# The merge's second branch evacuated inside its PSUM banks, not into SBUF tiles

## The chip, the cores and the metric

The kernel runs on one core of a Trainium2 chip. The metric is the device time of one execution in microseconds (us), the median over runs. The profile is taken by the hardware profiler from one execution. PE stands for TensorE, DVE for VectorE, ACT for ScalarE, POOL for GpSimd, SP for the queue that issues most DMAs. L1206 means line 1206 of the kernel before.

## The reference

Two layers of a hybrid backbone, all in fp32: 512 latent and 256 context tokens, 1024 model channels. Each layer has two parallel token mixers (a windowed attention A and a grouped-query attention B) that share one input projection. What matters here is the end of a layer, where both are merged:

```python
def _merge(a_att, b_att, a_z, b_z, g_a, g_b, w_o_a, w_o_b, w_out):
    o_a = (a_att * jax.nn.silu(a_z)) @ w_o_a
    o_b = (b_att * jax.nn.silu(b_z)) @ w_o_b
    merged = jax.nn.sigmoid(g_a) * o_a + jax.nn.sigmoid(g_b) * o_b
    return merged @ w_out
...
    out_x = _merge(a_att, b_att, a_z, b_z, g_a, g_b, w_o_a, w_o_b, w_out)
    x_new = x + gate_x * out_x
```

In layer 0 the context tokens go through the same merge; in layer 1 only the 512 latent tokens do. The output is the latent stream after layer 1.

## The kernel before, in words

**Products.** Every large product is made of fp32 operands that are split into a high and a low part (type fp32r): `hi` is a cast of the value, `lo` is the value minus `hi`. `mm3` then issues three matmuls for each block of 128 channels: hi by hi, and the two mixed products (L423, L424, L425). A product with a 512-column output over four blocks of channels is thus 12 matmuls, over eight blocks 24. `chan_proj` has a variant for operands that come late (L448, L449, L451): the products with the high part of the activations first, those with their low part behind them. Weights are loaded by SP into `raw` tiles; ACT casts them to `whi` (L393, L408), and DVE or POOL makes `wlo` (L396, L410), by turns.

**Merge.** The product with `w_o_b` has channels on the partitions: eight blocks f = 0 to 7, and for each the tokens in spans, 0 to 512 and 512 to 768 in layer 0 (16 chunks), 0 to 512 in layer 1 (8 chunks). Each chunk sums four blocks of input channels. The gate of branch B and the gated result of branch A (written in earlier chunks by `evac_a`, L694) lie in SBUF tiles `tg`; `tg_part(0, ...)` is A's, `tg_part(1, ...)` is B's. `evac_b` takes a chunk out of PSUM in four operations: L1206 on DVE multiplies the product by (1 + B's part), L1207 on DVE adds A's part, L1209 on ACT casts the sum to `mh`, L1210 on DVE subtracts to get `ml`. `mh` and `ml` are the operands of the product with `w_out`.

**Output.** That product has tokens on the partitions (six tiles of 128 tokens in layer 0, four in layer 1) and 512 columns at a time, in two halves n. `evac_o` multiplies it by the residual's gate (L1238) and adds it to the residual stream `xt` (L1240). In layer 1 the last tile's second half is made in two pieces of 256 columns (L1265 and L1267), each followed by its DMA out.

**PSUM.** In the merge six banks of 512 fp32 columns are used in turn: one named psf, five named psx (`psw` gives them out, psf at every sixth). A bank is given to its next chunk when the last operation that reads the old one is done. In layer 1 chunk 0 has psf, chunks 1 to 5 have psx, and chunk 6 has psf again.

**Order.** A scheduler orders the instructions of each engine from the program's text by its own estimate of times; each engine then takes its list strictly in turn and waits by semaphores. So an instruction that waits holds up all that stands behind it on its engine. What each engine does around the change is in the order rows below.

Of the kernel before, what the change touches and what calls it, by code (L numbers as in the profile page):

```python
# [7 lines left out]
F32 = mybir.dt.float32  # L8
# [4 lines left out]
ALU = mybir.AluOpType  # L13
# [38 lines left out]
def R(ap):  # L52
    return ap.bitcast(F32R)
# [7 lines left out]
def hybrid_kernel(es: ExitStack, tc, x, ctx, cvec, w_ada, w_ada0, small, gvec, w_in, w_o_a, w_o_b, w_out,  # L61
                  bias_int, bias_edge, rope, ident_d, out):
    nc = tc.nc
    V, S, G, T = nc.vector, nc.scalar, nc.gpsimd, nc.tensor
# [10 lines left out]
    def nm(s):  # L75
        uid[0] += 1
        return f"{s}_{uid[0]}"

    def big(name):
        return bigp.tile([128, 3072], F32, tag="big", name=nm(name))  # L80
# [12 lines left out]
    def open_ps(x=0, **kinds):  # L93

        if "es" in pm:
            pm["es"].close()
        pm["es"] = ExitStack()
        pm["n"], pm["i"], pm["v_for"] = x + 1, 0, ()
        if x:
            kinds["x"] = (x, 512)  # L100
        for kind, (bufs, cols) in kinds.items():
            ps_pool(pm["es"], kind, bufs, cols)
# [18 lines left out]
    def x_src(t):  # L121
        if t < 4:
            return x0[128 * t:128 * t + 128, :]
        return ctx0[(t - 4) * 128:(t - 3) * 128, :]
# [141 lines left out]
    def ada_steps(l, tiles, halves, nv, pool, queue=None):  # L266

        cb = {}

        def load(h):  # L270
            cb[h] = pool.tile([128, 2, 512], F32, tag="cb", name=nm("cb"), bufs=1)
            for v in range(nv):
                src = cd[8 * v + 4 * h:8 * v + 4 * h + 4].rearrange("k p -> (k p)").unsqueeze(0)
                nc.sync.dma_start(cb[h][:, v, :], src.to_broadcast([128, 512]))

        def load_tile(h, i):
            cb["w"] = pool.tile([128, 512], F32, tag="rawb", name=nm("rawb"), bufs=2)
            (queue or nc.sync).dma_start(cb["w"], w_ada[l, h, i])

        def dot(h, i, v):  # L280
            if v == 0:
                load_tile(h, i)
            w = cb["w"]
            o = w if v == nv - 1 else pool.tile([128, 512], BF16, tag="junk", name=nm("junk"), bufs=1)
            behind(ON_DVE, lambda: V.tensor_tensor_reduce(o, w, cb[h][:, v, :], 1.0, 0.0, ALU.mult, ALU.add,
                                                          asum[:, i, h, v:v + 1]))
        res = []
        for h in halves:
            res += [lambda h=h: load(h)] + [lambda h=h, i=i, v=v: dot(h, i, v) for i in tiles for v in range(nv)]
        return res  # L290
# [292 lines left out]
    def layer(l, hx, nxt, start):  # L583
# [67 lines left out]
        def hilo_tiles(name):  # L651
            return [big(name + part).rearrange("p (f n) -> p f n", f=4) for part in "hl"]

        def hilo(src, dst, fs, lo_eng=(G,), parts=((0, ntok),)):
            sv = src.rearrange("p (f n) -> p f n", f=4)
            for n0, n1 in parts:
                for f in fs:
                    S.copy(R(dst[0][:, f, n0:n1]), sv[:, f, n0:n1])
                    lo_eng[f % len(lo_eng)].tensor_tensor(R(dst[1][:, f, n0:n1]), sv[:, f, n0:n1], dst[0][:, f, n0:n1], ALU.subtract)
# [4 lines left out]
        def o_chunks(br, prepare, evac):  # L664

            src = (w_o_a if br == "a" else w_o_b)[l]
            act = lambda part, k: gated[br][part][:, k, :]
            res = []
            for i in range(4):
                st = {}  # L670

                def ld(i=i, st=st):
                    st["w"] = load_w2(src, 256 * i, 4, pool_lo if br == "b" and i == 0 else mix_lo)
                pieces = [lambda f=f, n0=n0, n1=n1, i=i, st=st:
                          chan_proj(st["w"], f, act, n0, n1, lambda f, a, b, ps: evac(2 * i + f, a, b, ps),
                                    3 if br == "b" and i == 0 and first else 0)
                          for f in range(2) for n0, n1 in spans]
                res.append((ld, ([prepare] if i == 0 and prepare else []) + pieces))
            return res
# [9 lines left out]
        def tg_part(c, f, n0, n1):  # L689
            return tg[2 * (f // 4) + c].rearrange("p (f n) -> p f n", f=4)[:, f % 4, n0:n1]  # L690
# [503 lines left out]
        with tc.tile_pool(name=f"mrg{l}", bufs=1, reuse_waits="tile") as mp:  # L1194
            open_ps(x=5)
            extra = lambda name: mp.tile([128, 3072], F32, tag="extra", name=nm(name))
            gv = mp.tile([128, nv, DM], F32, tag="gate", name=nm("gate"), bufs=1)
            for v in range(nv):
                src = gd[l][8 * v:8 * v + 8].rearrange("k p -> (k p)").unsqueeze(0)
                nc.sync.dma_start(gv[:, v, :], src.to_broadcast([128, DM]))  # L1200
            hilo(zb, gated["b"], [3], (V,), spans)
            mg = []

            def evac_b(f, n0, n1, ps):
                a, b = tg_part(0, f, n0, n1), tg_part(1, f, n0, n1)
                V.scalar_tensor_tensor(b, b, 1.0, ps, ALU.add, ALU.mult)  # L1206
                V.tensor_tensor(a, a, b, ALU.add)  # L1207
                hi, lo = [m[:, f % 4, n0:n1] for m in mg[f // 4]]
                S.copy(R(hi), a)  # L1209
                V.tensor_tensor(R(lo), a, hi, ALU.subtract)  # L1210
            chunks = o_chunks("b", None, evac_b)
            chunks[0][0]()
            for i in range(4):
                if i < 3:
                    chunks[i + 1][0]()
                if i % 2 == 0:
                    mg.append(hilo_tiles("m"))
                for piece in chunks[i][1]:
                    piece()

            nt = 6 if first else 4
            xv = [a.rearrange("p (t n) -> p t n", t=3) for a in (big("xt0"), extra("xt1"))]
            xts = []
            for t in range(nt):
                xt = xv[t // 3][:, t % 3, :]
                nc.sync.dma_start(xt, x_src(t) if first else xs1[128 * t:128 * t + 128, :])
                xts.append(xt)
            a_m = lambda part, k: mg[k // 4][part][:, k % 4, :]
            bg = ada_steps(1, range(16), (1,), 2, mp, G) + [lambda: ada_mod(1)] if first else []
            run(bg, 1)  # L1230
            per_bg = -(-len(bg) // nt)
            for n in range(2):
                w = load_w(w_out[l], 512 * n, 512, KT, mix_lo)

                def evac_o(t, ps, n=n):
                    cs = slice(512 * n, 512 * n + 512)
                    t1 = mp.tile([128, 512], F32, tag="t1", name=nm("t1"), bufs=2)
                    V.tensor_tensor(t1, ps, gv[:, 0 if t < 4 else 1, cs], ALU.mult)  # L1238
                    xt = xts[t]
                    V.tensor_tensor(xt[:, cs], xt[:, cs], t1, ALU.add)  # L1240
                    if not first:
                        nc.sync.dma_start(o_lat[16 * t:16 * t + 16][:, :, cs], xt[:, cs])
                    elif n == 1:
                        if t < 4:
                            G.dma_start(xs1[128 * t:128 * t + 128, :], xt)
                        late.append(lambda: make_hx(1, t, xt, nxt(), mp))
                late = []
                if first and n == 1:
                    hp["lag"] = 2
                for t in range(nt):  # L1250
                    if not first and n == 1 and t == nt - 1:
                        break
                    tok_proj(w, 512, a_m, t, evac_o)
                    run(bg, per_bg)
                    run(late, len(late))
                turn_late(0)
            if not first:

                for c0, c1 in ((0, 256), (256, 512)):
                    ws = [(hi[:, c0:c1], lo[:, c0:c1]) for hi, lo in w]  # L1260
                    cs = slice(512 + c0, 512 + c1)
                    ps = psw(c1 - c0)
                    tok_mm(ps, ws, c1 - c0, a_m, nt - 1, 0, KT)
                    t1 = mp.tile([128, 512], F32, tag="t1", name=nm("t1"), bufs=2)[:, :c1 - c0]
                    V.tensor_tensor(t1, ps, gv[:, 0, cs], ALU.mult)  # L1265
                    xt = xts[nt - 1]
                    V.tensor_tensor(xt[:, cs], xt[:, cs], t1, ALU.add)  # L1267
                    (nc.sync if c0 else S).dma_start(o_lat[16 * nt - 16:16 * nt][:, :, cs], xt[:, cs])


# [245 lines left out]
```

## Time and profile before

| | us |
|---|---|
| runs shown | 1102.42, 1097.99, 1101.49 |
| their median | 1101.49 |
| the profiled execution | 1097.34 |
| its span | 1095.5 |
| granted TensorE clock, mean | 1.0 |

| engine | busy us | share of the span |
|---|---|---|
| PE | 1066.4 | 97% |
| DVE | 757.7 | 69% |
| ACT | 613.6 | 56% |
| POOL | 438.5 | 40% |

A row of a timeline has the start of an instruction, its duration, the engine, the line, and output <- inputs by the names in the program; in brackets stands how long the engine was idle before it, and what released it. "x2" joins instructions of one kind. The duration of a matmul or a DVE operation includes its fill: two neighbours start closer together than one of them lasts (in the last merge DVE operations on 128x512 elements last 0.68 us and start 0.60 us apart). A group's row ends in "sum, mean ns | idle time before it, and what ended it". Where a wait is for a PSUM bank, the releaser is the last operation that read the bank before.

### The profile page before, as it was taken

To read this page: it belongs to the slowest core of one execution; us is meant where nothing else is said; L and a number is where in the kernel's file an instruction comes from. 1 tells how busy PE (TensorE), PEld (TensorE's weight loads), DVE (VectorE), ACT (ScalarE), POOL (GpSimd) and SP (SyncE) were. 2 spreads that over 40 slices of the span, in tenths; PEclk is the share of its full clock that TensorE was granted. 3 is DMA by queue.
4 is the path that set the end of the run, shared out by engine and by line. 5 is a ranking of instruction groups with operands and counts; after the bars stand their busy time and mean duration, and the time that the engine had idled before them with its cause. 6 is when DMAs were issued, how large, how long until landed. Compare 5 with 4: busy or idle time off the path is not lost. (4 is left out here: it accounts for less than half of the span.)

```text
span 1095.5 us, 17697 instructions
## 1 busy us (share of the span) xinstructions
PE 1066.4 (97%) x6032; PEld 882.3 (81%) x6032; DVE 757.7 (69%) x1630; ACT 613.6 (56%) x1256; POOL 438.5 (40%) x371
## 2 busy tenths in 40 slices
PE   8999999999999999998999999999999999999998
PEld 6688888788897888887788788888877888877777
DVE  5667889975388676665587885467997665677473
ACT  6464279777343477676141184444999346777420
POOL 1054235554247143354321445232455473444631
PEclk9999999999999999999999999999999999999999
DMA  9454325554544478789533542453455536889742
GB/s 371 159 172 148 92 66 110 130 144 115 166 147 128 122 180 215 164 256 239 198 114 108 182 131 72 136 163 105 127 146 129 152 107 170 192 261 225 201 154 77
DMA packets 236002, 171.83 MB, mean 157 GB/s; under 512 B 160140, under 2 KB 201864, under 8 KB 234248
## 3 DMA queue, kind: packets, MB, share of 16 engines
q1 hardware_dynamic: 228576, 156.31, 51.8%
q0 software_dynamic: 2368, 7.87, 2.3%
q10 hardware_dynamic: 4968, 6.53, 1.8%
q8 instruction: 47, 0.77, 0.3%
q14 instruction: 43, 0.35, 0.1%
HBM read 115.58 MB, written 17.32 MB: 121 GB/s over the span
## 5 line engine op out<-in xcount | busy, mean ns | idle before, releaser
L825 POOL TENSOR_TENSOR h<-p,h 128x256 f16<-128x256 f32 (+2 forms) x104 | 113.8, 1102 | 192.1 <-ACT h L824 141.5
L410 POOL TENSOR_TENSOR wlo<-raw,whi 128x512 fp32r<-128x512 f32 x70 | 97.3, 1392 | 132.2 <-ACT whi L408 113.0
L423 PE MATMUL psf<-hx,whi 128*128 128x512 f32 (+1 forms) x360 | 137.7, 382 | 1.6 <-DVE zt L614 1.2
L424 PE MATMUL psf<-hx,whi 128*128 128x512 f32 (+1 forms) x360 | 135.4, 376 | 0.0
L425 PE MATMUL psf<-hx,wlo 128*128 128x512 f32 (+1 forms) x360 | 135.3, 376 | 0.0
L408 ACT CAST whi<-raw 128x512 fp32r<-128x512 f32 x136 | 83.1, 621 | 73.6 <-DMA raw<-in_w_in_dram 50.5
L423 PE MATMUL psx<-whi,hx 128*128 128x512 f32 (+1 forms) x328 | 121.0, 372 | 0.0
L425 PE MATMUL psx<-whi,hx 128*128 128x512 f32 (+1 forms) x328 | 120.0, 367 | 0.0
L424 PE MATMUL psx<-wlo,hx 128*128 128x512 f32 (+1 forms) x328 | 119.7, 366 | 0.0
L396 POOL TENSOR_TENSOR wlo<-raw,whi 128x512 fp32r<-128x512 f32 x40 | 60.1, 1507 | 123.7 <-ACT whi L393 69.9
L393 ACT CAST whi<-raw 128x512 fp32r<-128x512 f32 x88 | 54.2, 623 | 91.7 <-PE psx L425 35.0
L496 POOL TENSOR_TENSOR ss<-ss,ehalf 128x8 f32<-128x8 f32 (+2 forms) x40 | 64.7, 1621 | 74.3 <-DVE ss L493 69.1
L824 ACT CAST h<-p 128x256 f16<-128x256 f32 (+2 forms) x136 | 81.5, 617 | 11.2 <-DMA vb<-h 4.8
L1154 DVE CUSTOM_DVE_ANT_0 p<-pss,vb 128x768 f32<-128x768 f32 x64 | 60.3, 954 | 31.0 <-PE pss L881 27.5
L423 PEld LDWEIGHTS psf<-hx,whi 128*128 128x128 f32 x360 | 67.8, 188 | 15.2 <-DVE zt L614 1.6
L410 DVE TENSOR_TENSOR wlo<-raw,whi 128x512 fp32r<-128x512 f32 x66 | 63.4, 963 | 23.6 <-ACT whi L408 23.3
L425 PEld LDWEIGHTS psf<-hx,wlo 128*128 128x128 f32 x360 | 67.8, 188 | 11.7
L424 PEld LDWEIGHTS psf<-hx,whi 128*128 128x128 f32 x360 | 67.9, 189 | 10.7
L1155 ACT ACTIVATE p<-pss,mx 128x768 f32<-128x768 f32 x64 | 57.6, 901 | 25.5 <-DVE mx L1154 25.1
L425 PEld LDWEIGHTS psx<-whi,hx 128*128 128x128 f32 x328 | 61.9, 189 | 10.2
L424 PEld LDWEIGHTS psx<-wlo,hx 128*128 128x128 f32 x328 | 62.0, 189 | 9.4
L423 PEld LDWEIGHTS psx<-whi,hx 128*128 128x128 f32 x328 | 61.8, 189 | 9.2 <-issue 0.2
(333 smaller groups left out, 2903.2 us busy)
## 6 DMA issues: line engine op xcount, KB each, us to landing
raw<-in_w_in_dram SPq DMA_DIRECT2D x168, 256.0 KB, 2.9
rawb<-in_w_ada_dram SPq DMA_DIRECT2D x48, 256.0 KB, 2.8
raw<-in_w_out_dram SPq DMA_DIRECT2D x32, 256.0 KB, 2.9
tg<-gs SPq DMA_DIRECT2D x4, 1536.0 KB, 8.8
rawx<-in_w_ada_dram SPq DMA_DIRECT2D x4, 1024.0 KB, 10.7
rawy<-in_w_ada_dram SPq DMA_DIRECT2D x4, 1024.0 KB, 9.4
gs<-zt ACTq DMA_DIRECT2D x16, 256.0 KB, 2.5
raw<-in_w_o_a_dram SPq DMA_DIRECT2D x16, 256.0 KB, 4.0
```

The costliest lines, as they stand in the source:

```text
L393: S.copy(hi[:, :n], raw[:, :n])
L396: e.tensor_tensor(lo[:, :n], raw[:, :n], F(hi[:, :n]), ALU.subtract)
L408: S.copy(hi, raw)
L410: lo_eng(i).tensor_tensor(lo, raw, F(hi), ALU.subtract)
L423: T.matmul(ps, lhs[0], rhs[0], start=first, stop=False)
L424: T.matmul(ps, lhs[0], rhs[1], start=False, stop=False)
L425: T.matmul(ps, lhs[1], rhs[0], start=False, stop=last)
L496: G.tensor_tensor(ss, ss, ehalf[:, :n], ALU.pow)
L824: S.copy(h[:, 0], p[:, :n])
L825: eng.tensor_tensor(h[:, 1], p[:, :n], h[:, 0], ALU.subtract)
L1154: V.tensor_tensor_reduce(p, pss, lift, -1.0, 3e38, ALU.add, ALU.min, mx[:, 0:1])
L1155: S.activation(p, pss, AF.Exp, bias=mx[:, 0:1], accum_out=r[:, i, e:e + 1])
```

## The change

`evac_b` no longer writes its results to the `tg` tiles in SBUF. L1206 writes the gated product back to the PSUM tile, L1207 adds A's part to it there, and the cast L1209 and the subtraction L1210 read the sum from there. In `evac_o` and in the two last pieces the product with the gate is written back to the PSUM tile, where a tile `t1` in SBUF was used, and the residual's addition reads it from there.

```diff
             def evac_b(f, n0, n1, ps):
                 a, b = tg_part(0, f, n0, n1), tg_part(1, f, n0, n1)
-                V.scalar_tensor_tensor(b, b, 1.0, ps, ALU.add, ALU.mult)
-                V.tensor_tensor(a, a, b, ALU.add)
+                V.scalar_tensor_tensor(ps, b, 1.0, ps, ALU.add, ALU.mult)
+                V.tensor_tensor(ps, ps, a, ALU.add)
                 hi, lo = [m[:, f % 4, n0:n1] for m in mg[f // 4]]
-                S.copy(R(hi), a)
-                V.tensor_tensor(R(lo), a, hi, ALU.subtract)
+                S.copy(R(hi), ps)
+                V.tensor_tensor(R(lo), ps, hi, ALU.subtract)
...
                 def evac_o(t, ps, n=n):
                     cs = slice(512 * n, 512 * n + 512)
-                    t1 = mp.tile([128, 512], F32, tag="t1", name=nm("t1"), bufs=2)
-                    V.tensor_tensor(t1, ps, gv[:, 0 if t < 4 else 1, cs], ALU.mult)
+                    V.tensor_tensor(ps, ps, gv[:, 0 if t < 4 else 1, cs], ALU.mult)
                     xt = xts[t]
-                    V.tensor_tensor(xt[:, cs], xt[:, cs], t1, ALU.add)
+                    V.tensor_tensor(xt[:, cs], ps, xt[:, cs], ALU.add)
...
                     tok_mm(ps, ws, c1 - c0, a_m, nt - 1, 0, KT)
-                    t1 = mp.tile([128, 512], F32, tag="t1", name=nm("t1"), bufs=2)[:, :c1 - c0]
-                    V.tensor_tensor(t1, ps, gv[:, 0, cs], ALU.mult)
+                    V.tensor_tensor(ps, ps, gv[:, 0, cs], ALU.mult)
                     xt = xts[nt - 1]
-                    V.tensor_tensor(xt[:, cs], xt[:, cs], t1, ALU.add)
+                    V.tensor_tensor(xt[:, cs], ps, xt[:, cs], ALU.add)
```

The scheduler gives another order at some places. In the rows, "waits DVE_49" is a wait on DVE's semaphore, and the number behind a name tells tiles apart. First, TensorE in layer 0, where the first branch's last product (psf_6046, with weights of `w_o_a`) ends and the second branch's chunks follow. Before:

```order
L425 MATMUL psf_6046<-gah_5411,wlo_5824 128x256
L423 MATMUL psx_6309<-gbh_6064,whi_6166 128x256 [waits DVE_49]
L424 MATMUL psx_6309<-gbl_6065,whi_6166 128x256
L425 MATMUL psx_6309<-gbh_6064,wlo_6168 128x256
...
L423 MATMUL psx_6340<-gbh_6064,whi_6248 128x512 [waits DVE_49]
L424 MATMUL psx_6340<-gbl_6065,whi_6248 128x512
L425 MATMUL psx_6340<-gbh_6064,wlo_6250 128x512
```

With the change:

```order
L425 MATMUL psf_6046<-gah_5411,wlo_5824 128x256
L448 MATMUL psf_6178<-gbh_6064,whi_6154 128x512 [waits DVE_49]
L449 MATMUL psf_6178<-gbh_6064,wlo_6156 128x512
...
L451 MATMUL psf_6178<-gbl_6065,whi_6154 128x512 x2
...
L425 MATMUL psf_6178<-gbh_6064,wlo_6162 128x512
L423 MATMUL psx_6309<-gbh_6064,whi_6166 128x256 [waits DVE_49]
L424 MATMUL psx_6309<-gbl_6065,whi_6166 128x256
L425 MATMUL psx_6309<-gbh_6064,wlo_6168 128x256
```

The chunk in bank psf with the late order (psf_6178, L448 to L425, 12 matmuls) now comes right behind the first branch's last product, and the 256-column chunk psx_6309 behind it; before, psx_6309 and others stood between.

Second, DVE at the same place; psx_6195, psx_6212 and so on are chunks of the second branch, psx_6195 the first of them, and psx_6309 takes its bank. Before:

```order
L694 SCALAR_TENSOR_TENSOR tg_5423<-tg_5423,psf_6046 128x256 [waits PE_49]
L410 TENSOR_TENSOR wlo_6336<-raw_6332,whi_6334 128x512 [waits DMAHW6_49,Activation_49]
L1206 SCALAR_TENSOR_TENSOR tg_6060<-tg_6060,psx_6309 128x256 [waits PE_49]
L1207 TENSOR_TENSOR tg_5421<-tg_5421,tg_6060 128x256 [waits DVE_49]
L1206 SCALAR_TENSOR_TENSOR tg_6062<-tg_6062,psx_6340 128x512 [waits PE_49]
L1207 TENSOR_TENSOR tg_5423<-tg_5423,tg_6062 128x512 [waits DVE_49]
L1206 SCALAR_TENSOR_TENSOR tg_6060<-tg_6060,psf_6178 128x512 [waits PE_49]
L396 TENSOR_TENSOR wlo_6497<-raw_6493,whi_6495 128x512 [waits DMAHW4_49,Activation_49,Pool_49]
L1207 TENSOR_TENSOR tg_5421<-tg_5421,tg_6060 128x512 [waits DVE_49]
L1206 SCALAR_TENSOR_TENSOR tg_6062<-tg_6062,psx_6357 128x256 [waits PE_49]
L1210 TENSOR_TENSOR ml_6177<-tg_5421,mh_6176 128x256
```

With the change:

```order
L694 SCALAR_TENSOR_TENSOR tg_5423<-tg_5423,psf_6046 128x256 [waits PE_49]
L410 TENSOR_TENSOR wlo_6336<-raw_6332,whi_6334 128x512 [waits DMAHW6_49,Activation_49]
L1206 SCALAR_TENSOR_TENSOR psf_6178<-tg_6060,psf_6178 128x512 [waits DVE_49,PE_49]
L396 TENSOR_TENSOR wlo_6497<-raw_6493,whi_6495 128x512 [waits DMAHW4_49,Activation_49,Pool_49]
L1207 TENSOR_TENSOR psf_6178<-psf_6178,tg_5421 128x512 [waits DVE_49]
L1210 TENSOR_TENSOR ml_6177<-psx_6195,mh_6176 128x256
L1210 TENSOR_TENSOR ml_6177<-psx_6212,mh_6176 128x512
L1210 TENSOR_TENSOR ml_6177<-psx_6229,mh_6176 128x256
L1210 TENSOR_TENSOR ml_6177<-psx_6258,mh_6176 128x512
L1210 TENSOR_TENSOR ml_6177<-psx_6275,mh_6176 128x256
L1210 TENSOR_TENSOR ml_6177<-psf_6178,mh_6176 128x512 [waits Activation_49]
L1206 SCALAR_TENSOR_TENSOR psx_6309<-tg_6060,psx_6309 128x256 [waits DVE_49,PE_49]
```

Six L1210s now stand together, ahead of psx_6309's L1206. Ahead of the first of them stand L1206, L396 and L1207, the latter two with psf_6178's L1206 in the same sequence as before.

Third, DVE in layer 1's merge. The seventh chunk's bank (psf_11513 before, psf_11501 with the change) is that of the first chunk (psf_11385 before, psf_11373 with the change); TensorE's own order is the same up to the output projection. Before:

```order
L1206 SCALAR_TENSOR_TENSOR tg_11290<-tg_11290,psf_11385 128x512 [waits DMAHW6_49,PE_49]
L1206 SCALAR_TENSOR_TENSOR tg_11290<-tg_11290,psx_11402 128x512 [waits PE_49]
L1207 TENSOR_TENSOR tg_10838<-tg_10838,tg_11290 128x512 [waits DVE_49]
L1206 SCALAR_TENSOR_TENSOR tg_11290<-tg_11290,psx_11431 128x512 [waits PE_49]
L396 TENSOR_TENSOR wlo_11575<-raw_11571,whi_11573 128x512 [waits DMAHW3_49,Activation_49]
L1206 SCALAR_TENSOR_TENSOR tg_11290<-tg_11290,psx_11448 128x512 [waits PE_49]
L1207 TENSOR_TENSOR tg_10838<-tg_10838,tg_11290 128x512 [waits DVE_49]
L1206 SCALAR_TENSOR_TENSOR tg_11292<-tg_11292,psx_11479 128x512 [waits DMAHW2_49,PE_49]
L1206 SCALAR_TENSOR_TENSOR tg_11292<-tg_11292,psx_11496 128x512 [waits PE_49]
L1207 TENSOR_TENSOR tg_10838<-tg_10838,tg_11290 128x512 [waits DVE_49]
L396 TENSOR_TENSOR wlo_11587<-raw_11583,whi_11585 128x512 [waits DMAHW5_49,Activation_49]
L1210 TENSOR_TENSOR ml_11384<-tg_10838,mh_11383 128x512 [waits Activation_49]
```

With the change:

```order
L1206 SCALAR_TENSOR_TENSOR psf_11373<-tg_11278,psf_11373 128x512 [waits DMAHW6_49,PE_49]
L1206 SCALAR_TENSOR_TENSOR psx_11390<-tg_11278,psx_11390 128x512 [waits PE_49]
L1207 TENSOR_TENSOR psf_11373<-psf_11373,tg_10826 128x512 [waits DVE_49]
L1206 SCALAR_TENSOR_TENSOR psx_11419<-tg_11278,psx_11419 128x512 [waits PE_49]
L396 TENSOR_TENSOR wlo_11563<-raw_11559,whi_11561 128x512 [waits DMAHW3_49,Activation_49]
L1206 SCALAR_TENSOR_TENSOR psx_11436<-tg_11278,psx_11436 128x512 [waits PE_49]
L1207 TENSOR_TENSOR psx_11390<-psx_11390,tg_10826 128x512 [waits DVE_49]
L1206 SCALAR_TENSOR_TENSOR psx_11467<-tg_11280,psx_11467 128x512 [waits DMAHW2_49,PE_49]
L1206 SCALAR_TENSOR_TENSOR psx_11484<-tg_11280,psx_11484 128x512 [waits PE_49]
L1207 TENSOR_TENSOR psx_11419<-psx_11419,tg_10826 128x512 [waits DVE_49]
L396 TENSOR_TENSOR wlo_11575<-raw_11571,whi_11573 128x512 [waits DMAHW5_49,Activation_49]
L1210 TENSOR_TENSOR ml_11372<-psf_11373,mh_11371 128x512 [waits Activation_49]
```

The sequence of lines is the same in these twelve rows; the first of them was the last reader of the first chunk's bank, and with the change that is the last of them. In the output projection of layer 1, TensorE's first products now come token by token, without the first matmul of the second half's first weight among them.

## The prediction

> **What bounds the kernel now.** I read the page's totals first, then the busy time by stage (the stage marks are mine: layer 0's merge starts within 540–580 us, layer 1's merge is 1034–1062 and the rest of its output projection follows), then TensorE's waits in the last merge.
>
> ```profile
> PE 1066.4 (97%) x6032; PEld 882.3 (81%) x6032; DVE 757.7 (69%) x1630; ACT 613.6 (56%) x1256; POOL 438.5 (40%) x371
> ```
> ```profile
> core 0: us, PE busy (x) PEld busy (x) DVE busy (x) ACT busy (x) POOL busy (x), PEclk, DMA share, GB/s
> 540.00:580.00 40.00, 40.00 (x218) 34.74 (x218) 30.65 (x55) 13.65 (x26) 7.61 (x5) 1.00 0.31 106
> 580.00:640.00 60.00, 59.46 (x268) 48.41 (x268) 48.22 (x104) 16.50 (x35) 23.09 (x33) 1.00 0.40 132
> 700.00:860.00 160.00, 156.42 (x795) 126.17 (x794) 121.47 (x298) 108.07 (x222) 61.49 (x60) 1.00 0.49 134
> 1034.00:1062.00 28.00, 25.56 (x117) 20.51 (x112) 19.73 (x30) 10.10 (x17) 10.62 (x4) 1.00 0.51 179
> ```
> ```profile
> engine line waited for: us in total, times, longest us
> PE psf L424 <- POOL wlo L396: 1.7, 1, 1.7
> PE psf L423 <- ACT gbh L658: 0.7, 1, 0.7
> ```
>
> TensorE is the bound everywhere. In layer 0's merge it has no idle time at all, and DVE is busy 30.65 of 40 us beside it: work taken from DVE there saves nothing. In layer 1's merge TensorE idles 28.00 − 25.56 = 2.44 us, of which 1.7 is a wait for a weight's low half from POOL and 0.7 for the gated activations, which the edit doesn't touch. So in the two merges the most that a cheaper evacuation can earn is 1.7 us, while anything that makes TensorE wait for a bank is paid in full.
>
> **What the change moves.** No instruction is added or removed; each of the four operations of `evac_b` stays, and so do the two of `evac_o`. What moves is the moment a PSUM bank comes free. Six banks serve the merge (one f, five x). Before, a bank is free after L1206, the first operation, since the sum then lives in the tile of SBUF. After, L1207, L1209 and L1210 read the bank, so it is free only after L1210, the last. A wait of TensorE on a bank therefore becomes a wait on the fourth operation of the chunk that held it six chunks earlier, and on all that stands ahead of that operation on DVE.
>
> The time from a DVE release to the waiting matmul is needed first: DVE, then TensorE.
>
> ```profile
> 535.56 0.67 DVE L694 SCALAR_TENSOR_TENSOR tg<-tg,psf 128x512 f32<-128x512 f32 x1
> ```
> ```profile
> 536.29 0.39 PE L423 MATMUL psf<-gah,whi 128*128 128x256 f32 x1 [2.15 <-DVE tg L694]
> ```
>
> 535.56 + 0.67 = 536.23, the matmul starts at 536.29: 0.06 us.
>
> **Layer 0.** TensorE's order changes: the first branch's last product (psf) is now followed by the chunk whose low activations come late (L448 to L451), which takes the same f bank; before, a 256-column x chunk followed it.
>
> ```profile
> 548.57 0.28 PE L425 MATMUL psf<-gah,wlo 128*128 128x256 f32 x1
> 548.69 0.28 PE L423 MATMUL psx<-gbh,whi 128*128 128x256 f32 x1
> ...
> 553.47 0.40 PE L448 MATMUL psf<-gbh,whi 128*128 128x512 f32 x1
> ...
> 555.99 0.39 PE L425 MATMUL psf<-gbh,wlo 128*128 128x512 f32 x1
> 556.22 0.28 PE L425 MATMUL psx<-gbh,wlo 128*128 128x256 f32 x1
> ```
> ```profile
> 548.97 0.41 DVE L694 SCALAR_TENSOR_TENSOR tg<-tg,psf 128x256 f32<-128x256 f32 x1
> ...
> 556.42 0.69 DVE L1206 SCALAR_TENSOR_TENSOR tg<-tg,psf 128x512 f32<-128x512 f32 x1 [1.93 <-PE psf L425]
> 557.02 1.03 DVE L396 TENSOR_TENSOR wlo<-raw,whi 128x512 fp32r<-128x512 f32 x1
> 557.97 0.68 DVE L1207 TENSOR_TENSOR tg<-tg,tg 128x512 f32<-128x512 f32 x1
> 558.58 0.41 DVE L1206 SCALAR_TENSOR_TENSOR tg<-tg,psx 128x256 f32<-128x256 f32 x1
> ```
>
> First wait: TensorE could go on at 548.69, but the f bank is free after L694, 548.97 + 0.41 = 549.38, so the late chunk starts at 549.44: 0.75 us. Its twelve matmuls take 556.22 − 553.47 = 2.75 us, so its last starts 2.52 in, at 551.96, and TensorE is ready for the next chunk at 552.19. Second wait: that chunk needs the bank of the second branch's first chunk, whose release is now its L1210. DVE's order puts L1206 of the late chunk, one L396 and L1207 of the late chunk ahead of it. The quoted rows have just these three in a row: from the last matmul's start (555.99) to the slot behind them (558.58) 2.59 us. So L1210 starts at 551.96 + 2.59 = 554.55, a 256-column one takes 0.41, and TensorE resumes at 554.55 + 0.41 + 0.06 = 555.02: 2.83 us. After that five more L1210s stand together on DVE at under 0.7 each, and each chunk on TensorE takes 1.4 to 2.75, so no third wait. Layer 0: 0.75 + 2.83 = +3.6. Behind the waiting matmul stand all later chunks and products of the layer. If the weight behind that L396 comes no earlier than before, the wait grows; if L1210 were served ahead of it, it would shrink by 1.0.
>
> **Layer 1.** TensorE's order is the same up to the output projection, so the wait is read straight off DVE's order. The seventh chunk takes the f bank of the first.
>
> ```profile
> 1039.86 0.39 PE L423 MATMUL psf<-gbh,whi 128*128 128x512 f32 x1
> ...
> 1057.58 0.50 PE L424 MATMUL psf<-wlo,mh 128*128 128x512 f32 x1 [1.70 <-POOL wlo L396]
> ```
> ```profile
> 1037.79 0.69 DVE L1206 SCALAR_TENSOR_TENSOR tg<-tg,psf 128x512 f32<-128x512 f32 x1 [1.48 <-DMA gate<-gd]
> 1038.39 0.68 DVE L1206 SCALAR_TENSOR_TENSOR tg<-tg,psx 128x512 f32<-128x512 f32 x1
> 1038.99 0.69 DVE L1207 TENSOR_TENSOR tg<-tg,tg 128x512 f32<-128x512 f32 x1
> 1039.59 0.68 DVE L1206 SCALAR_TENSOR_TENSOR tg<-tg,psx 128x512 f32<-128x512 f32 x1
> 1040.19 1.29 DVE L396 TENSOR_TENSOR wlo<-raw,whi 128x512 fp32r<-128x512 f32 x1
> 1041.40 0.67 DVE L1206 SCALAR_TENSOR_TENSOR tg<-tg,psx 128x512 f32<-128x512 f32 x1
> 1042.00 0.68 DVE L1207 TENSOR_TENSOR tg<-tg,tg 128x512 f32<-128x512 f32 x1
> 1042.60 1.27 DVE L1206 SCALAR_TENSOR_TENSOR tg<-tg,psx 128x512 f32<-128x512 f32 x2
> 1043.79 0.68 DVE L1207 TENSOR_TENSOR tg<-tg,tg 128x512 f32<-128x512 f32 x1
> 1044.40 0.68 DVE L396 TENSOR_TENSOR wlo<-raw,whi 128x512 fp32r<-128x512 f32 x1
> 1045.00 1.78 DVE L1210 TENSOR_TENSOR ml<-tg,mh 128x512 fp32r<-128x512 f32 x1
> ```
> ```profile
> 1040.40 0.61 ACT L1209 CAST mh<-tg 128x512 fp32r<-128x512 f32 x1
> ```
>
> Before, L1206 of the first chunk ended at 1038.48, ahead of 1039.86, and nobody waited. After, the release is L1210 of that chunk, which is the twelfth operation of the same list in both orders: it starts at 1045.00 (its cast is done by 1041.0) and, at the 0.68 of its neighbours, ends at 1045.68. TensorE resumes at 1045.74: 1045.74 − 1039.86 = +5.88. Behind it wait the last two chunks and the whole output projection.
>
> The next banks come in time: their L1210s are the 15th and 17th of DVE's list, at its 0.60 pitch done by about 1047.5 and 1048.7, while TensorE wants them one and two chunks after 1045.74, at 1048.5 and 1051.2. The sums themselves are due later still: by the same counting the last low half is there near 1056.5, and the projection reaches it three chunks' matmuls (33 at 2.75/12 us) after 1051.2, near 1058.8.
>
> Against this stands the 1.70 us wait for POOL. In the new order the output projection takes its first products token by token and no longer asks for the second half's first weight at that place, so the weight has over ten us more and the wait goes. Layer 1: 5.88 − 1.70 = +4.2.
>
> **The output's part** (`evac_o`) I cost at nothing: the bank is held for one operation more.
>
> ```profile
> 1062.22 0.69 DVE L1238 TENSOR_TENSOR t<-psx,gate 128x512 f32<-128x512 f32 x1 [5.82 <-PE psx L425]
> 1062.95 0.69 DVE L1240 TENSOR_TENSOR xt<-xt,t 128x512 f32<-128x512 f32 x1
> ```
>
> That is 0.73 us, under a rotation of six banks at 24 matmuls (5.5 us) each; without that cover it would cost 0.73 a token. At the very end the same two operations stand in series as before.
>
> **Unknown: what a DVE operation costs that writes PSUM.** No row of before has one. The nearest are reads of PSUM and operations within SBUF:
>
> ```profile
> L1206 DVE SCALAR_TENSOR_TENSOR tg<-tg,psx 128x512 f32<-128x512 f32 x11 | 7.4, 678 | 1.5 <-PE psx L425 1.5
> ...
> L1207 DVE TENSOR_TENSOR tg<-tg,tg 128x512 f32<-128x512 f32 x16 | 12.0, 749 | 0.0
> ```
>
> The best 512-column ones of either take 0.68, with a pitch of 0.60. Low end: L1207's mean falls to 678 once it has a PSUM operand, −0.07 on the four L1207s ahead of the two waits: −0.3. High end: reading and writing the same bank don't overlap and the columns pass twice. 256 columns end 0.28 earlier than 512 (0.41 against 0.69), so 512 columns are about 0.55; nine PSUM operations stand ahead of layer 1's release and two ahead of layer 0's, 11 × 0.55 = +6.0. I take the row that is nearest, 0: L1206 already reads PSUM at the speed of SBUF. [...]
>
> **Sum.** 3.6 + 4.2 = +7.8. The profiled execution (span 1095.50, time 1097.34) would be 1105.1; the median of the runs shown, 1101.49, lies 4.15 above it, so the time is 1101.49 + 7.8 = **1109.3 us**.
>
> **Rivals.** (1) Not slower: the banks don't bind, and only the POOL wait goes. POOL shows why its weight was late:
>
> ```profile
> 1051.04 7.73 POOL L396 TENSOR_TENSOR wlo<-raw,whi 128x512 fp32r<-128x512 f32 x2 [4.81 <-ACT whi L393]
> ```
>
> Two subtractions take 7.73 us while DVE's own L396 at 1044.40, one subtraction of the same size, took 0.68. [...] This decides only if L1210 of the first chunk ends before 1039.86, that is, if at most two operations stood ahead of it; eleven do. It gives 1101.49 − 1.7 = 1099.8. (2) Given back: layer 0's 3.6 is taken up by idle time later in layer 1, 160.00 − 156.42 = 3.58 in 700–860, if what TensorE waits for there isn't itself delayed. Against it: nothing in the row says that those waits are for work that is independent of TensorE's earlier products, and what depends on them is late by as much. It gives 1101.49 + 4.2 = 1105.7. The 0.54 idle in 580–640 alone gives 1108.8, within my forecast. (3) In-place writes at the double price: 1109.3 + 6.0 = 1115.3; the price decides from about 0.2 us more per operation, which takes the sum past 1111.5.
>
> **How the numbers follow.** A difference under 0.5% (5.5 us) can't be told from none here, the runs of before alone span 4.4: slower means above 1107.0, faster below 1096.0. The forecast has 0.62, with 1106 to 1111.5 as its own range; (1) 0.10, (2) 0.16, (3) 0.12. Slower: (3) and nine tenths of the forecast and a little of (2), 0.70; same: (1), most of (2) and the rest, 0.26; faster needs more than the idle time of both merges, 0.04. The range 1102 to 1115 leaves out (1) and the upper part of (3).
>
> **What would show it.** TensorE idle of about 5.9 us at the seventh chunk of layer 1, released by DVE L1210, and of 0.75 (by L694) and 2.8 us (by L1210) in layer 0; no POOL wait of 1.7 near the first weights of the second half; `evac_b` operations with PSUM in and out at 0.68. The prediction is wrong if L1206 or L1207 takes well over 0.7 (then (3)), if DVE reaches L1210 earlier than its order says, or if TensorE's waits add to 7.8 and the span grows by less (then (2)).

## The result, and the profile after

The changed kernel takes 1111.9 us (median of 6 runs, 1107.46 to 1113.86), the kernel before in the same comparison 1100.77 us (6 runs, 1097.99 to 1102.42). The ratio is 1.0100 with a 95% interval of 1.0082 to 1.0118: slower by 11.1 us. Forecast were +7.8 us and 1109.3 us. The measured time lies inside the stated 1102 to 1115, but just above 1106 to 1111.5, the forecast's own range within it.

The page's totals and the busy time by stage of the changed kernel; the columns are those of the table before.

```profile
PE 1072.5 (97%) x6032; PEld 887.0 (80%) x6032; DVE 752.8 (68%) x1630; ACT 613.3 (55%) x1256; POOL 432.2 (39%) x371
```
```profile
core 0: us, PE busy (x) PEld busy (x) DVE busy (x) ACT busy (x) POOL busy (x), PEclk, DMA share, GB/s
540.00:580.00 40.00, 36.42 (x188) 31.44 (x187) 24.20 (x48) 10.71 (x21) 5.14 (x4) 0.91 0.28 100
...
1040.00:1075.00 35.00, 28.59 (x142) 22.51 (x141) 21.22 (x34) 8.84 (x15) 3.83 (x3) 0.95 0.44 142
```

DVE has less to do (752.8 against 757.7) and POOL too, and the kernel is slower: both merges have idle time on TensorE that they hadn't, and PEclk, 1.00 in every row quoted of before, is 0.91 and 0.95. TensorE's waits, first around layer 0's merge, then around layer 1's:

```profile
PE psx L423 <- DVE ml L1210: 3.0, 1, 3.0
PE psf L423 <- DVE tg L694: 2.2, 1, 2.2
PE psf L448 <- DVE tg L694: 0.6, 1, 0.6
```
```profile
PE psf L423 <- DVE ml L1210: 5.7, 1, 5.7
PE psf L423 <- ACT gbh L658: 0.7, 1, 0.7
```

The three forecast waits are there, released by the operations that were named; the wait of 1.7 us for POOL is gone. These idle times count from the modelled end of the matmul ahead. Counted as the forecast counts, from the moment at which the next matmul could have started (0.12 us behind a start at 553.03, 0.23 behind starts at 556.50 and 1049.68), the three waits are 0.73, 3.17 and 5.83 us, and POOL's of before is 1.86. The wait on L694 of 2.2 us in the first list is there in every kernel, before included. DVE around layer 0's two waits, and TensorE's waiting matmuls with what follows them:

```profile
553.41 0.41 DVE L694 SCALAR_TENSOR_TENSOR tg<-tg,psf 128x256 f32<-128x256 f32 x1
553.88 1.15 DVE L410 TENSOR_TENSOR wlo<-raw,whi 128x512 fp32r<-128x512 f32 x1
556.92 0.70 DVE L1206 SCALAR_TENSOR_TENSOR psf<-tg,psf 128x512 f32<-128x512 f32 x1 [1.90 <-PE psf L425]
558.23 0.69 DVE L396 TENSOR_TENSOR wlo<-raw,whi 128x512 fp32r<-128x512 f32 x1 [0.60 <-ACT whi L393]
558.84 0.69 DVE L1207 TENSOR_TENSOR psf<-psf,tg 128x512 f32<-128x512 f32 x1
559.44 2.27 DVE L1210 TENSOR_TENSOR ml<-psx,mh 128x256 fp32r<-128x256 f32 x5
```
```profile
559.90 0.39 PE L423 MATMUL psx<-gbh,whi 128*128 128x256 f32 x1 [3.02 <-DVE ml L1210]
...
562.20 0.63 PE L423 MATMUL psx<-gbh,whi 128*128 128x512 f32 x1
562.62 0.63 PE L424 MATMUL psx<-gbl,whi 128*128 128x512 f32 x1
...
565.73 0.28 PE L423 MATMUL psx<-gbh,whi 128*128 128x256 f32 x1
```

L1206, L396, L1207, L1210 stand as the order had them. What wasn't foreseen is behind the wait: matmuls of 512 columns last 0.63 us and start 0.42 us apart, where the quoted ones of before take 2.75 us for twelve, 0.23 apart. The same in layer 1, where DVE reaches the first chunk's L1210 as its twelfth operation:

```profile
1047.85 0.70 DVE L1206 SCALAR_TENSOR_TENSOR psf<-tg,psf 128x512 f32<-128x512 f32 x1 [1.48 <-DMA gate<-gd]
...
1054.41 0.68 DVE L396 TENSOR_TENSOR wlo<-raw,whi 128x512 fp32r<-128x512 f32 x1
1055.01 0.68 DVE L1210 TENSOR_TENSOR ml<-psf,mh 128x512 fp32r<-128x512 f32 x1
```
```profile
1055.74 0.79 PE L423 MATMUL psf<-gbh,whi 128*128 128x512 f32 x1 [5.67 <-DVE ml L1210]
1056.34 0.63 PE L424 MATMUL psf<-gbl,whi 128*128 128x512 f32 x1
...
1060.02 0.40 PE L423 MATMUL psx<-gbh,whi 128*128 128x512 f32 x1
```

The twelve matmuls of the seventh chunk take 1060.02 − 1055.74 = 4.28 us; the granted clock is 0.50 from 1055.40 to 1058.81 and 1.00 behind that. At before's twelve in 2.75 this is 1.5 us more.

### The profile page after: what moved, and what is told of

Read it like the earlier page. It is cut to its first block, busy times and chain, and to the rows that moved or that the text cites. A ratio compares the mean times of both kernels' runs of the same rounds, so it can differ in the third digit from the quotient of the medians.

```text
span 1111.0 us, 17696 instructions
## 1 busy us (share of the span) xinstructions
PE 1072.5 (97%) x6032; PEld 887.0 (80%) x6032; DVE 752.8 (68%) x1630; ACT 613.3 (55%) x1256; POOL 432.2 (39%) x371
## 5 line engine op out<-in xcount | busy, mean ns | idle before, releaser
L410 POOL TENSOR_TENSOR wlo<-raw,whi 128x512 fp32r<-128x512 f32 x70 | 98.9, 1416 | 134.0 <-ACT whi L408 115.5
L425 PE MATMUL psf<-hx,wlo 128*128 128x512 f32 (+1 forms) x360 | 135.3, 376 | 0.0
L425 PE MATMUL psx<-whi,hx 128*128 128x512 f32 (+1 forms) x328 | 120.2, 367 | 0.0
L396 POOL TENSOR_TENSOR wlo<-raw,whi 128x512 fp32r<-128x512 f32 x40 | 53.6, 1341 | 142.3 <-ACT whi L393 94.5
L425 PEld LDWEIGHTS psf<-hx,wlo 128*128 128x128 f32 x360 | 67.8, 188 | 11.7
L425 PEld LDWEIGHTS psx<-whi,hx 128*128 128x128 f32 x328 | 61.9, 189 | 10.2 <-issue 0.2
```

The source lines that it names most:

```text
L396: e.tensor_tensor(lo[:, :n], raw[:, :n], F(hi[:, :n]), ALU.subtract)
L410: lo_eng(i).tensor_tensor(lo, raw, F(hi), ALU.subtract)
L425: T.matmul(ps, lhs[1], rhs[0], start=False, stop=last)
```

## The experiments

Three theories stand in the expectations. H: banks held longer make TensorE wait, and each long wait is followed by a stretch at a lower clock. C: only the waits cost. W: writing PSUM in place is itself what costs. Ratios are to the kernel before, on the same chip.

**The output's part alone.** `evac_b` as before:

```diff
-                V.scalar_tensor_tensor(ps, b, 1.0, ps, ALU.add, ALU.mult)
-                V.tensor_tensor(ps, ps, a, ALU.add)
+                V.scalar_tensor_tensor(b, b, 1.0, ps, ALU.add, ALU.mult)
+                V.tensor_tensor(a, a, b, ALU.add)
                 hi, lo = [m[:, f % 4, n0:n1] for m in mg[f // 4]]
-                S.copy(R(hi), ps)
-                V.tensor_tensor(R(lo), ps, hi, ALU.subtract)
+                S.copy(R(hi), a)
+                V.tensor_tensor(R(lo), a, hi, ALU.subtract)
```

> evac_b as before, only the output's part (evac_o and the last two pieces) in PSUM. Theory H (a bank is held until L1210 instead of L1206, TensorE waits for it, and after a wait of about 3 us or more its granted clock is near half for some 3.4 us, which costs about 1.6 us more each time): no wait is added, since the bank is held 0.73 us longer under a rotation of 6 x 5.5 us; ratio 1.000 (0.998 to 1.002), the 1.7 us wait for POOL's low half stays because the products are again taken by weight block. Theory W (writing PSUM in place from DVE is itself what costs, by slower DVE operations or by slower matmuls beside them): this has 19 x 2 of the changed operations, so slower by a share of the 11 us, 1.002 to 1.004.

Measured: 1100.62 us, ratio 0.9991 (0.9975 to 1.0007). No bank wait was added and the wait for POOL stayed, here from this kernel's list of TensorE's waits:

```profile
PE psf L424 <- POOL wlo L396: 1.7, 1, 1.7
```

So the output's part shows no cost, as H has it; W's 1.002 lies above the interval.

**One layer at a time.** The new `evac_b` under `if first:` or `if not first:`, the old one in the other layer; the output's part changed in both.

> The new evac_b in layer 0 alone, evac_o in PSUM in both. Theory H: layer 0's two waits, 0.6 + 3.0 us, and 1.7 us for the matmuls at the lower clock behind the second: +5.3 us, ratio 1.0048; layer 1 as before with its 1.7 us wait for POOL. Theory C (only the waits cost; the slow matmuls behind them are chance, as the ones near 540 us in the changed kernel's profile): +3.6 us, 1.0033. Theory W: two thirds of the changed chunks are here (16 of 24), about +7 us, 1.0065.

> The new evac_b in layer 1 alone, evac_o in PSUM in both. Theory H: one wait of 5.7 us, 1.6 us at the lower clock behind it, less the 1.7 us wait for POOL: +5.6 us, ratio 1.0051. Theory C: +4.0 us, 1.0036. Theory W: 8 of 24 chunks, about +4 us with no wait needed. Together with the kernel that has it in layer 0 alone, H wants +10.9 us, C +7.6.

Measured: layer 0 alone 1107.37 us, 1.0060 (1.0042 to 1.0077), layer 1 alone 1107.38 us, 1.0061 (1.0040 to 1.0081). Each layer shows its own waits and not the other's; first the kernel with the change in layer 0, then the one with it in layer 1 (the branches of the `if` move the numbers of the lines by one: L1211 is the subtraction L1210):

```profile
PE psx L423 <- DVE ml L1211: 3.1, 1, 3.1
...
PE psf L448 <- DVE tg L694: 0.6, 1, 0.6
```
```profile
PE psf L423 <- DVE ml L1211: 5.7, 1, 5.7
```

Both cost more than their waits alone (3.6 and 4.0 us), +6.6 and +6.7 by the ratios (5.8 each by the medians, with 1101.54 for the kernel before), and both intervals hold H's value; C's lies below layer 0's interval and just below layer 1's. Layer 0's loss isn't given back later. W's 1.0065 fits layer 0 too, but its 4 us for layer 1 (1.0036) lies below the interval: its shares (16 chunks to 8) don't fit equal losses. The two losses add to 13.3 us by the ratios and 11.7 by the medians, where H wanted 10.9 and C 7.6; the changed kernel's is 11.1.

**The bank freed after the second operation.**

```diff
                 V.scalar_tensor_tensor(ps, b, 1.0, ps, ALU.add, ALU.mult)
-                V.tensor_tensor(ps, ps, a, ALU.add)
+                V.tensor_tensor(a, ps, a, ALU.add)
                 hi, lo = [m[:, f % 4, n0:n1] for m in mg[f // 4]]
-                S.copy(R(hi), ps)
-                V.tensor_tensor(R(lo), ps, hi, ALU.subtract)
+                S.copy(R(hi), a)
+                V.tensor_tensor(R(lo), a, hi, ALU.subtract)
```

> L1206 writes PSUM in place as in the changed kernel, but L1207 reads PSUM and writes the sum to A's tile in SBUF, from where L1209 and L1210 read it: the bank is free after the second operation. Theory H: in layer 1 L1207 of the first chunk ends near 1039.7, just ahead of TensorE's wish at 1039.86, so no wait over 0.3 us; layer 0 has the order of before and no wait; the 1.7 us for POOL go or stay: ratio 0.9985 to 1.001, no matmul at a lower clock in the merges. Theory W: the in-place writes of all 24 chunks are still there, so a good part of the 1% stays, 1.004 or more.

Measured: 1102.36 us, 1.0010 (0.9994 to 1.0025). All 24 chunks still write PSUM in place, and the 1% is gone: W falls. In its profile TensorE waits for no bank of the second branch; the wait on L694 that every kernel has is there, and behind it the clock is at half for 3.4 us (the mean granted clock of this execution is 0.993, that of the kernel before's 1.000), which the expectation had ruled out for the merges. The wait of 1.7 us for POOL is gone too, replaced by one of 0.6 us:

```profile
PE psf L423 <- ACT gbh L658: 0.7, 1, 0.7
PE psx L425 <- DVE ml L1210: 0.6, 1, 0.6
```

**Spare matmuls in the waits.** The first version has them in layer 1's wait, the second in layer 0's too, placed behind the late chunk. Their results are read by nobody; all else is the changed kernel. `behind` fixes their place on TensorE.

```diff
+        if hp.pop("spare", False):
+            sb = psw(512, "t")[:, :n1 - n0]
+
+            def spare():
+                for k in range(24):
+                    T.matmul(sb, wh(k % 4, 0), act(k % 4, 0), start=True, stop=True)
+                mm3(ps, (wh(0, 0), wh(0, 1)), (act(0, 0), act(0, 1)), True, False)
+            behind(ON_PE, spare, hp.pop("spare_after", None))
...
+                    if not first and i == 3 and j == 0:
+                        hp["spare"] = True
+                    if first and i == 1 and j == 3:
+                        hp["spare"], hp["spare_after"] = True, late_end
                     piece()
+                    if first and i == j == 0:
+                        late_end = latest(ON_PE, 1)
```

> The changed kernel with 24 spare matmuls (5.45 us, into a bank that nobody reads) ahead of layer 1's seventh chunk, that is, in the place of its 5.7 us wait. Theory H: TensorE isn't idle, keeps its clock, and the seventh chunk's 12 matmuls take 2.7 us instead of 4.28: 1.6 us faster than the changed kernel, ratio 1.0086 to before. Rival M (the matmuls behind the wait are slow because DVE reads and writes PSUM at the same time): they stay at 4.3 us, ratio 1.010.

> The changed kernel with spare matmuls in both long waits: 24 of 256 columns (2.9 us, in layer 0) and 24 of 512 (5.45 us, in layer 1), into a bank that nobody reads. The waits stay as long, but TensorE isn't idle in them. Theory H: both stretches at the lower clock go, 3.2 us faster than the changed kernel on the same chip: 1.0071; in the profile the 12 matmuls behind either wait take 1.45 us (256 columns) and 2.7 us (512). Theory C: no faster than the changed kernel.

> The changed kernel again, beside the one with both waits filled and on the same chip. Theory H: 1.0100 (1.008 to 1.012): waits of 0.6 + 3.0 + 5.7 us, less POOL's 1.7, are 7.6 us, and two stretches at the lower clock of about 1.6 us each make 10.8. Theory C (waits only): 7.6 us, 1.0069.

Measured: layer 1 filled 1109.58 us, 1.0078 (1.0057 to 1.0100); both filled 1109.56 us, 1.0076 (1.0061 to 1.0092); the changed kernel again, beside the latter, 1111.47 us, 1.0089 (1.0067 to 1.0112). With both filled it is 1.9 us faster than the changed kernel beside it, where H wanted 3.2. The direction is H's, but the intervals overlap: by the times alone C isn't excluded. The traces decide. Layer 1 with spare matmuls:

```profile
1046.91 5.60 PE L452 MATMUL pst<-gbh,whi 128*128 128x512 f32 x24
1052.77 0.50 PE L423 MATMUL psf<-gbh,whi 128*128 128x512 f32 x1 [0.26 <-DVE ml L1221]
...
1055.63 0.39 PE L423 MATMUL psx<-gbh,whi 128*128 128x512 f32 x1
```

and layer 0 of the kernel with both filled:

```profile
555.60 3.03 PE L452 MATMUL pst<-gbh,whi 128*128 128x256 f32 x24
558.58 0.39 PE L423 MATMUL psx<-gbh,whi 128*128 128x256 f32 x1
...
560.11 0.40 PE L423 MATMUL psx<-gbh,whi 128*128 128x512 f32 x1
...
562.85 0.28 PE L423 MATMUL psx<-gbh,whi 128*128 128x256 f32 x1
```

The seventh chunk of layer 1 takes 1055.63 − 1052.77 = 2.86 us instead of 4.28. Layer 0's next 24 matmuls take 562.85 − 558.58 = 4.27 us instead of 565.73 − 559.90 = 5.83. DVE goes on with the same kinds of operations in PSUM behind the release in both; what differs is TensorE's idleness, so the rival that DVE's traffic slows the matmuls falls. The stretch behind an idle wait costs 1.4 to 1.6 us in these two places. In the two other executions with the wait of 5.67 us it costs more: there the seventh chunk takes 5.11 us (layer 1 alone, 1055.56 − 1050.45) and 5.28 us (changed, again, 1060.61 − 1055.33), that is, 2.3 and 2.4 us more than 2.86.

A stage that one profile shows without the rest of the execution confirms it: from the matmul that waits 0.74 us for the gated activations, ahead of layer 1's merge, to the end of the span.

| kernel | starts | span | us | bank wait in it |
|---|---|---|---|---|
| before | 1035.64 | 1095.5 | 59.86 | none |
| output's part alone | 1034.15 | 1094.1 | 59.95 | none |
| layer 0 alone | 1047.16 | 1107.1 | 59.94 | none |
| freed after L1207 | 1044.83 | 1104.0 | 59.17 | none |
| layer 1 filled | 1042.68 | 1106.6 | 63.92 | 0.26, filled |
| both filled | 1043.94 | 1107.9 | 63.96 | 0.3, filled |
| changed | 1045.69 | 1111.0 | 65.31 | 5.67 |
| changed, again | 1045.26 | 1111.6 | 66.34 | 5.67 |
| layer 1 alone | 1040.36 | 1106.6 | 66.24 | 5.67 |

The wait alone, less POOL's, would make 59.86 + 5.67 − 1.70 = 63.83. The two filled kernels are there, at 63.9 and 64.0; the three that idle lie 1.5 to 2.5 us above it. In the traces the granted clock is at half behind the wait until 1058.81 (changed), 1060.64 (changed, again) and 1055.34 (layer 1 alone), that is, for 3.07, 5.31 and 4.89 us; half of each is 1.5, 2.7 and 2.4 us, which is about what the stage lost.

**More banks, and another order.** Layer 1's last two chunks were given the two PSUM banks that the merge leaves unused (`psw(n1 - n0, "t")` for i = 3), once in the changed kernel and once with layer 0's `evac_b` as before. In a third kernel DVE's order in layer 1 was forced, L1206 of chunk k behind L1210 of chunk k−2:

```diff
-            mg = []
+            mg, done = [], []
...
-                V.scalar_tensor_tensor(ps, b, 1.0, ps, ALU.add, ALU.mult)
+                if first or f < 2:
+                    V.scalar_tensor_tensor(ps, b, 1.0, ps, ALU.add, ALU.mult)
+                else:
+                    behind(ON_DVE, lambda: V.scalar_tensor_tensor(ps, b, 1.0, ps, ALU.add, ALU.mult), done[f - 2])
...
                 V.tensor_tensor(R(lo), ps, hi, ALU.subtract)
+                done.append(latest(ON_DVE, 1))
```

> The changed kernel with layer 1's seventh and eighth chunk in the two banks that the merge leaves unused (pst), so that none of the eight chunks of layer 1 waits for another's bank. Theory H: layer 1's wait, the lower clock behind it and the wait for POOL go, layer 0's +5.3 us stay: +3.6 us, ratio 1.0033. Theory W: the operations are the same, so 1.010.

> Layer 0 with evac_b as before, layer 1 with the new evac_b and its last two chunks in the unused banks, evac_o in PSUM in both. Theory H: no bank wait is left and POOL's 1.7 us wait is gone: 1.7 us faster than before, ratio 0.9985 (0.997 to 1.000). Theory W: slower, 1.003.

> The changed kernel with DVE's order in layer 1 forced: L1206 of chunk k stands behind L1210 of chunk k-2, so the first chunk's L1210 is the 7th of DVE's list instead of the 12th, behind two L1206, two L1207 and two L396. Theory H: the bank comes near 1042 by the times of before, 1.5 to 2.5 us late instead of 5.7, and the clock may hold: with layer 0's 5.3 and without POOL's 1.7 it is +5.1 to +6.5 us, ratio 1.0046 to 1.006. Theory W: 1.010.

Measured: the banks in the changed kernel 1110.71 us, 1.0083 (1.0065 to 1.0101); with layer 0 as before 1104.92 us, 1.0036 (1.0019 to 1.0052); the forced order 1110.79 us, 1.0078 (1.0056 to 1.0100). All three expectations of H were too low. In the two with banks the wait had moved on: no chunk waits, but the output projection's first product comes next in the rotation, takes the first chunk's bank, and its L1210 now stands behind eight L1206. The waiting matmul in the changed kernel with banks, then in the one with layer 0 as before:

```profile
1057.20 0.80 PE L423 MATMUL psf<-whi,mh 128*128 128x512 f32 x1 [4.79 <-DVE ml L1210]
```
```profile
1051.88 0.80 PE L423 MATMUL psf<-whi,mh 128*128 128x512 f32 x1 [4.79 <-DVE ml L1211]
```

With 1.6 for the clock and without POOL's 1.7 this is +4.7 us for the latter; +4.0 was measured. In the forced order the wait shrank, but the clock fell behind it as well (L1213 is the subtraction here):

```profile
1054.68 0.50 PE L423 MATMUL psf<-gbh,whi 128*128 128x512 f32 x1 [2.58 <-DVE ml L1213]
```

L1210 came 3.1 us earlier after the first L1206 (1053.95 − 1049.86 = 4.09 there, 1055.01 − 1047.85 = 7.16 in the changed kernel), and the wait is shorter by as much (5.67 − 2.58), which is H's mechanism in its size; the mean clock over the 4 us behind it is still 0.64. By the stage of the table above this kernel takes 1110.2 − 1047.69 = 62.51 us, 1.8 more than 59.86 + 2.58 − 1.70, with 3.41 us at half clock behind the wait. No kernel of these beats the one before: the best two are the same as it.

## Why the prediction was right, and which term it lacked

- **Where it is bound:** right. DVE and POOL got less work and nothing was earned by that.
- **Layer 0, two waits, 0.75 + 2.83 = 3.6:** measured 0.73 + 3.17 = 3.9, counted in the same way (0.56 + 3.02 of idle time). L396 ran in 0.69 instead of 1.03 but waited 0.60 for its cast, as the text had allowed.
- **Layer 1, 5.88 less 1.70:** measured 5.83 (5.67 of idle time) and no wait for POOL. No third bank wait followed in either layer.
- **The output's part at nothing:** shown by the kernel with that part alone.
- **A DVE operation that writes PSUM:** taken at no extra cost. The groups of the changed kernel, in which the mean of one stands behind the comma:

```profile
L1207 DVE TENSOR_TENSOR psx<-psx,tg 128x512 f32<-128x512 f32 x11 | 7.5, 689 | 0.0
L1206 DVE SCALAR_TENSOR_TENSOR psx<-tg,psx 128x512 f32<-128x512 f32 x11 | 7.5, 688 | 2.1 <-PE psx L425 2.1
L1210 DVE TENSOR_TENSOR ml<-psx,mh 128x512 fp32r<-128x512 f32 x11 | 7.3, 680 | 1.3 <-ACT mh L1209 1.3
```

  L1206 rose from 678 to 688 ns, L1207 fell from 749 (a mean that single ones of up to 1.78 us had raised) to 689: no double price, and rival (3) is out.
- **The term that was missing:** the sum "3.6 + 4.2" sized the waits and let TensorE go on behind them at its former pace ("Its twelve matmuls take … 2.75 us", "TensorE resumes at 1045.74"). The granted clock is 0.50 from 560.47 to 563.88, 0.57 us behind TensorE's restart in layer 0, and from 1055.40 to 1058.81 around its restart in layer 1. The two stretches measure 1.56 us in layer 0 (5.83 − 4.27) and 1.5 in layer 1 (4.28 − 2.75), so 3.9 + 5.83 − 1.86 + 3.1 = 11.0, against 11.1 measured with an interval of 9.0 to 13.0. The row of before that misled is the 2.15 us wait on L694, behind which the clock stayed at 1.00.
- **The number:** 1111.9 lies above the 1111.5 at which the text let rival (3) begin. The stated range held it because it had room for that rival, which didn't come: that part is luck. That it is slower, and most of the amount, rests on the waits and isn't.
- **Rivals:** (1) didn't come, as eleven operations stood ahead. POOL did run without the delay: in the merge of the changed kernel its subtractions take 1.27 and 1.30 us, and the median of its forty is 1.30 (the longest took 6.49 us before and 1.75 now). They also run at other times than before, and no run shows why two of them took 7.73 us in the kernel before.

```profile
1049.68 1.27 POOL L396 TENSOR_TENSOR wlo<-raw,whi 128x512 fp32r<-128x512 f32 x1 [5.88 <-PE psx L425]
1062.12 1.30 POOL L396 TENSOR_TENSOR wlo<-raw,whi 128x512 fp32r<-128x512 f32 x1 [11.17 <-ACT whi L393]
```

  (2) didn't come: the change in layer 0 alone costs 6.6 us at the end by the ratio.

The two profiled executions differ by 15.5 us (1111.0 − 1095.5), more than the medians. 4.4 us of that lie ahead of any wait that the change adds (553.41 against 548.97 for the same L694); 2.9 of them are there when the earlier wait on L694 ends (539.19 against 536.29), and their cause stays open; the rest fits the half clock behind that wait, which the last section shows.

## What to carry to other kernels

Freeing a PSUM bank early was worth more here, where TensorE is the bound, than a saved tile in SBUF: count how many operations stand on the evacuating engine's list ahead of the one that now frees the bank, and compare with when TensorE wants it. A wait of TensorE is to be priced with the slow matmuls that can follow it, here another 1.5 to 2.5 us behind the waits of 3.02 and 5.67 us; of 48 waits of 1.26 to 2.01 us two had a lower clock behind them. And a bank wait removed at one user can pass to the next in the rotation, as it did here to the output projection's first product (4.79 us), unless the release itself comes earlier.

## What the runs showed of the hardware

In these traces a wait of TensorE was followed by a stretch at half clock, or by nothing, and in a middle range of lengths both happened. By the granted clock, as a mean over the 4 us behind each wait of over 1.25 us in all twelve profiled executions (before, changed, ten experiments), from 100 us on:

| idle before | waits | clock fell (0.50 to 0.71) |
|---|---|---|
| 1.26 to 2.01 | 48 | 2 |
| 2.13 to 2.15 (on L694) | 12 | 8 |
| 2.47 and 2.56 | 2 | 1 |
| 2.58 to 5.67 | 12 | 12 |

The traces' clock tells the middle rows apart. In each of the twelve executions the changes of the granted clock all lie on one grid of 3.413 us (in the changed kernel 539.99, 543.40, 560.47, 563.88, 1055.40, 1058.81, 1110.02), and the grid's place against the program differs between executions: in the two of the changed kernel the wait of 5.67 us ends 0.34 us (1055.74 − 1055.40) and 1.51 us (1055.33 − 1053.82) behind the last edge. The wait on L694 is in every kernel alike. Here are the steps of the grid around it, first in the kernel before, where an edge cuts the wait in two (1.27 and 0.88 us) and the clock holds, then in the changed one, where the whole wait lies in one step and the next step is at half clock:

```profile
core 0: us, PE busy (x), PEclk, DMA share, GB/s
532.00:535.42 3.42, 2.14 (x13) 1.00 0.97 373
535.42:538.83 3.41, 2.54 (x18) 1.00 0.67 260
538.83:542.24 3.41, 3.41 (x20) 1.00 0.00 0
```
```profile
536.58:539.99 3.41, 1.26 (x9) 1.00 1.02 403
539.99:543.40 3.41, 3.41 (x14) 0.50 0.24 90
```

In the eight executions in which the clock fell behind L694 the wait lies in one step, but for 0.02 us in one of them; in the four in which it held, it is split, with 1.14 to 1.62 us in the longer part. Over all steps of the twelve executions that start at full clock, from 100 us to the last matmul, TensorE's idle time by the matmul rows tells nearly every case: 21 steps were idle for 62% or more (2.1 us) and the next was at half clock in all 21; 3458 were idle for 56% or less and the next was at half clock in three, at 42 to 45%, whose cause stays open. By these counts the slow matmuls behind the waits aren't chance as theory C has it, but a wait of 2.6 to 3.1 us could be split by an edge too; the seven here weren't.

The clock came back at an edge as well. A step at half clock that was idle for 10% or less was followed by full clock each time; the three that were idle for 37% or more, because the wait reached into them, were followed by a second step at half clock. That fits the wait of 5.67 us, which cost 1.5 us once and 2.4 to 2.5 twice. The rows of the changed kernel's second execution:

```profile
1050.40:1053.82 3.42, 0.00 (x0) 1.00 0.49 153
1053.82:1057.23 3.41, 1.91 (x5) 0.50 0.33 93
1057.23:1060.64 3.41, 3.41 (x10) 0.50 0.97 356
```

The matmuls around L694's wait in the changed kernel show a step at half clock:

```profile
539.19 0.38 PE L423 MATMUL psf<-gah,whi 128*128 128x256 f32 x1 [2.15 <-DVE tg L694]
...
540.01 0.41 PE L423 MATMUL psf<-gah,whi 128*128 128x256 f32 x1
...
543.41 0.28 PE L424 MATMUL psx<-gbl,whi 128*128 128x256 f32 x1
```

From 540.01 to 543.41 matmuls of 256 columns start 0.21 apart, before and after it 0.12. Behind L694 such a stretch came in eight of the twelve executions and not in four. At about 1.5 us each, stretches that come in one run and not in another may be a part of what runs of one kernel differ by (4.4 us before, 6.4 changed); that is an estimate. The mean granted clock of the changed kernel's six runs lies between 0.992 and 0.996.
